# Longer steps in the second group: 16 ticks before the last attention products of six heads, ten between retention steps

## The chip, the cores and the metric

The kernel runs on one core of a Trainium2 chip. The metric is the device time of one execution in microseconds (us). A core has five engines with a queue of their own: TensorE (PE, with its weight loads as PEld), VectorE (DVE), ScalarE (ACT), GpSimd (POOL) and SyncE (SP), which here only issues transfers. Each engine takes its instructions in order; semaphores make it wait for another.

## The reference

One step of a layer with two groups of eight heads, head size 128, on 1024 prompt rows and 8 streams of 16 sample rows with 1024 cached rows each. All is in 32 bits.

```python
q_sb, k_sb, v_sb, gate_sb, q_r, k_r, v_r, gate_r = project(rms_norm(x), w_in)   # 2048 x 8192, rope on q_r, k_r
# stick-breaking attention: z = q k^T / sqrt(128), strictly causal
a = exp(log_sigmoid(z) + later)        # later: sum of log_sigmoid(-z) over the keys that follow
o_sb = a @ v
# retention: chunks of 64, a state s per head
o_r = (q k^T * intra) @ v + (q @ s) * decay_read
s = s * exp(lg * n) + k^T @ (decay_write * v)
y = concat(head_rms_norm(o_sb) * silu(gate_sb), head_rms_norm(o_r) * silu(gate_r))
x = x + rms_norm(y @ w_out)
```

It returns the new rows of x, the new keys and values, and the retention states.

## The kernel before

**Groups and panels.** The prompt's rows are eight tiles of 128. The first group takes tiles 0 to 3 and the sample rows, the second tiles 4 to 7. In each group a loop goes over the eight heads; a head has panels: queries, keys and gate of retention (`ret_queries`, `ret_keys`, `ret_gate`), queries and keys of attention and, for two heads at a time, its values (`attention`), and the gate (`gates`). Every weight block comes as `wr` through SP (L215, L271 for row panels, L1020 for the output), is split by ScalarE (L131, `wh`) and VectorE (L132, `wl`) into two parts, and is used in three products (L229, L288 in row panels, L1030 to L1032 in the output). In the second group a panel has 48 products of 128x512 and a row panel 192 of 128x256. After the groups come four output panels for three chunks of row tiles; the first of them still runs with ticks.

**Jobs and ticks.** All other work is in jobs, Python generators that run beside the panels. After each product of a panel (each three of a row panel, four times after each tile's three products in the first output panel) `tick()` raises a clock by one and lets at most one job do its next step: the one that is due. What a step yields is the number of ticks until the job is due again. `drain(job)` ticks without products until a job is done.

```python
def tick():
    clock[0] += 1
    for job in jobs:
        if job.at <= clock[0]:
            wait = step(job)
            ...
            job.at = clock[0] + wait
```

The constants D_... hold these numbers, mostly as pairs for the two groups (`phase[0]` is 0 or 1). The ticks fix the order in which the program is written down; a scheduler may still move an instruction within its engine's order, so that one which isn't ready stands a little later.

**The attention job** (`stick_breaking`, L562 to L623) takes a head's four row tiles through six steps. Step s makes the scores of row s (L588, into rotating PSUM banks), sigmoids on ScalarE (L500, L501), masks on GpSimd (L506), the scan and the multiplication on VectorE (L517, L518), and sends `be` to DRAM block by block (L474). One step later it is read back (L481), so that the blocks are exchanged; two steps later VectorE transposes within the blocks (L578). Then come the products with the values (L618, one pair of passes for each of the row's tiles, into the one PSUM bank `pa`), a copy (L621) and a sum of squares (L538). In steps 4 and 5, which make no scores, a yield of D_TR ticks (L612) stands between the transpose of row 2 or 3 (t = 6 or 7, seven or eight tiles) and its products. In the second group the job also has D_NAT 11, D_TB 24 and D_AV 11 ticks in its steps. `finish` scales the rows and turns them through DRAM (L474 on ScalarE's queue, L481 on SP's), 23 and 13 ticks apart.

**The retention job** (`ret_branch`, `retention`, L747 to L800) turns the keys the same way (L474, L481, L851), and then takes four chunks. For each: scores of the next chunk (L754, `rs`) and their decay on VectorE (L756, `sc`), products with the values and with the state (L772, L777, into `pa`), two combining instructions (L780, L781); then, D_RET ticks later, the product for the new state (L787, `pS`) and its update on VectorE (L792); and D_RET ticks later the next chunk. So there are nine yields of D_RET in the second group.

```python
sc = scores(0, 0)
yield D_RET[phase[0]]
for i in range(4):
    nxt = scores(i + 1, 0)
    ...
    yield D_RET[phase[0]]
    ...
    yield D_RET[phase[0]]
```

**The end of a job.** The next head drains the retention job after its retention queries' panel, and the attention job after its attention queries' panel (the last head both after the first output panel). In heads 5 to 7 of the second group the panels come in another order: heads 5 and 6 have attention earlier, and head 7 begins with it; the time until the drain is 256 ticks for the attention jobs of heads 4 and 5, and 304 for those of heads 0 to 3 and 6.

**The seam.** At the start of the second group the decode job of the first group's last head, which attends to the cached rows (L661, L728 with values from `vc`, L689), ends beside the first retention of the second group.

## Time and profile before

| what | us |
|---|---|
| median of three runs (2395.4 to 2400.91) | 2400.34 |
| the profiled execution | 2397.79 |
| its span, first to last instruction | 2396.1 |
| its TensorE busy / VectorE / ScalarE / GpSimd | 2332.6 / 1254.6 / 919.6 / 646.2 |
| mean granted TensorE clock | 0.993 of full |

A row of the timeline has the start in us, the duration, the engine, the line, the operation, the tiles (written<-read), the shape and the count of equal instructions that follow each other; in brackets, how long the engine was idle before it and what ended that. A row of the table by stretches has the stretch, its length, each engine's busy time and instructions in the order PE, PEld, DVE, ACT, POOL, then the granted clock, the share of the DMA engines' time and GB/s. A row of waits has the waiting line, what it waited for, the sum in us, how often, and the longest.

### The profile page before, as it was taken

To read this page: it belongs to the slowest core of one execution; us is meant where nothing else is said; L and a number is where in the kernel's file an instruction comes from. 1 tells how busy PE (TensorE), PEld (TensorE's weight loads), DVE (VectorE), ACT (ScalarE), POOL (GpSimd) and SP (SyncE) were. 2 spreads that over 40 slices of the span, in tenths; PEclk is the share of its full clock that TensorE was granted. 3 is DMA by queue.
4 is the path that set the end of the run, shared out by engine and by line. 5 is a ranking of instruction groups with operands and counts; after the bars stand their busy time and mean duration, and the time that the engine had idled before them with its cause. 6 is when DMAs were issued, how large, how long until landed. Compare 5 with 4: busy or idle time off the path is not lost.

```text
span 2396.1 us, 40529 instructions
## 1 busy us (share of the span) xinstructions
PE 2332.6 (97%) x14832; PEld 2094.6 (87%) x14832; DVE 1254.6 (52%) x2442; ACT 919.6 (38%) x1937; POOL 646.2 (27%) x1033
## 2 busy tenths in 40 slices
PE   7999999999999999998899999999999999999998
PEld 7998899999999999987778888889898888888887
DVE  7245455445554555455545554555554566564544
ACT  6323333324333333324333343343343444444443
POOL 3144353444344353443302111120220220010000
PEclk9999999999999999999999999999999999999999
DMA  7658879797889879798875555556654667765553
GB/s 244 166 130 210 167 166 197 174 199 164 188 178 191 181 174 187 182 192 199 188 189 150 150 141 150 146 142 153 153 152 127 166 163 195 231 214 181 189 191 131
DMA packets 677050, 418.68 MB, mean 175 GB/s; under 512 B 224753, under 2 KB 620017, under 8 KB 674545
## 3 DMA queue, kind: packets, MB, share of 16 engines
q1 hardware_dynamic: 524272, 285.99, 47.6%
q0 software_dynamic: 32256, 71.36, 13.7%
q10 hardware_dynamic: 120320, 58.74, 9.0%
q8 instruction: 116, 1.90, 0.3%
q14 instruction: 86, 0.70, 0.1%
HBM read 336.24 MB, written 79.69 MB: 174 GB/s over the span
## 4 chain that ended last, share of the span: by engine, by line
PE 83%; DMA 7%; DVE 4%; issue 2%; ACT 2%; SPq 1%; POOL 0%; DVEq 0%; ACTq 0%; POOLq 0%
PE acc L229 44%; PE accn L288 17%; DMA mr<-s_y 4%; PE a L1031 3%; PE a L1032 3%; PE a L1030 3%; PE pa L618 3%; PE z L588 2%; DMA wr<-w_in 2%; PE zc L661 1%; PE pd L728 1%; DMA mr<-s_h 1%; DVE wl L132 1%; DVE ml L132 1%; ACT mh L131 1%
## 5 line engine op out<-in xcount | busy, mean ns | idle before, releaser
L229 PE MATMUL acc<-mh,wh 128*128 128x256 f32 (+2 forms) x2304 | 665.4, 342 | 7.8 <-ACT wh L131 5.0
L132 DVE TENSOR_TENSOR wl<-wr,wh 128x512 fp32r<-128x512 f32 (+1 forms) x576 | 391.8, 685 | 523.8 <-ACT wh L131 513.8
L229 PE MATMUL acc<-ml,wh 128*128 128x384 f32 (+2 forms) x2304 | 663.8, 341 | 0.0
L229 PE MATMUL acc<-mh,wl 128*128 128x256 f32 (+2 forms) x2304 | 660.2, 339 | 0.6 <-DVE wl L132 0.5
L131 ACT ACTIVATE wh<-wr 128x512 fp32r<-128x512 f32 (+1 forms) x576 | 357.4, 625 | 730.9 <-PE acc L229 247.7
L229 PEld LDWEIGHTS acc<-mh,wh 128*128 128x128 f32 x2304 | 420.7, 189 | 45.0 <-ACT wh L131 7.1
L229 PEld LDWEIGHTS acc<-mh,wl 128*128 128x128 f32 x2304 | 424.7, 189 | 31.6 <-issue 2.1
L229 PEld LDWEIGHTS acc<-ml,wh 128*128 128x128 f32 x2304 | 422.9, 189 | 33.2 <-issue 5.3
L645 POOL DMA_DIRECT2D kc<-cache_sb_k x512 | 331.6, 653 | 370.0 <-DVE kcT L683 205.9
L288 PE MATMUL accn<-whn,mh 128*128 128x256 f32 x1152 | 329.2, 287 | 0.6 <-ACT whn L131 0.5
L288 PE MATMUL accn<-wln,mh 128*128 128x256 f32 x1152 | 325.9, 283 | 1.5 <-DVE wln L132 1.5
L288 PE MATMUL accn<-whn,ml 128*128 128x256 f32 x1152 | 325.9, 283 | 0.0
L288 PEld LDWEIGHTS accn<-whn,mh 128*128 128x128 f32 x1152 | 220.5, 192 | 10.5 <-issue 7.5
L288 PEld LDWEIGHTS accn<-wln,mh 128*128 128x128 f32 x1152 | 220.9, 192 | 2.5 <-DVE wln L132 1.7
L288 PEld LDWEIGHTS accn<-whn,ml 128*128 128x128 f32 x1152 | 220.9, 192 | 0.0
L1031 PE MATMUL a<-wl,mh 128*128 128x512 f32 (+1 forms) x576 | 219.5, 381 | 0.2 <-DVE wl L132 0.2
L1032 PE MATMUL a<-wh,ml 128*128 128x512 f32 (+1 forms) x576 | 219.0, 381 | 0.0
L1030 PE MATMUL a<-wh,mh 128*128 128x512 f32 (+1 forms) x576 | 218.9, 381 | 0.0
L132 DVE TENSOR_TENSOR wln<-wrn,whn 128x512 fp32r<-128x512 f32 x128 | 87.5, 687 | 119.7 <-ACT whn L131 119.5
L131 ACT ACTIVATE whn<-wrn 128x512 fp32r<-128x512 f32 x128 | 80.1, 633 | 151.6 <-PE accn L288 65.4
L481 POOL DMA_DIRECT2D be<-s_be x128 | 94.0, 741 | 134.2 <-DMA s_be<-be 114.6
L1031 PEld LDWEIGHTS a<-wl,mh 128*128 128x128 f32 x576 | 108.4, 188 | 21.2 <-DVE wl L132 0.9
(189 smaller groups left out, 2611.6 us busy)
## 6 DMA issues: line engine op xcount, KB each, us to landing
wr<-w_in SPq DMA_DIRECT2D x384, 256.0 KB, 4.2
wr<-w_out SPq DMA_DIRECT2D x184, 256.0 KB, 3.6
wrn<-w_in SPq DMA_DIRECT2D x128, 256.0 KB, 3.2
kc<-cache_sb_k POOLq DMA_DIRECT2D x512, 64.0 KB, 4.6
vc<-cache_sb_v SPq DMA_DIRECT2D x64, 512.0 KB, 8.5
xt<-x_prompt SPq DMA_DIRECT2D x8, 1024.0 KB, 6.2
xr<-x_prompt SPq DMA_DIRECT2D x8, 1024.0 KB, 6.5
out<-out ACTq DMA_DIRECT2D x24, 256.0 KB, 3.6
```

Source lines behind the costliest of these rows:

```text
L131: nc.scalar.activation(hi, src, AF.Copy)
L132: nc.vector.tensor_tensor(lo, src, hi.bitcast(F32), ALU.subtract)
L229: last = nc.tensor.matmul(a[:, :m], lhs[:, j, :], rhs[w][:, j, o : o + m], start=(w == 0 and j == 0 and n == 0), stop=(w == KT // WQ - 1 a ...
L288: anchor[0] = nc.tensor.matmul(a, lhs[q][:, jj, ts], rhs[:, j, :], start=(w == 0 and j == 0 and n == 0 and t % 2 == 0), stop=(w == KT // 2 ...
L481: q.dma_start(raw[32 * i : 32 * i + 32, :].rearrange("p (k a) -> p k a", a=32), s[:, :, 32 * i : 32 * i + 32].rearrange("k (j b) a -> b (k ...
L588: nc.tensor.matmul(z[:, :c], q2[a][:, i * P : (i + 1) * P], k2[b][:, s : s + c], start=(m == 0), stop=(m == 2),)
L618: nc.tensor.matmul(po[:, :P], at[:, j, :], vn[:, j, :], start=(j == 0), stop=(j == t))
L645: nc.gpsimd.dma_start(kc[32 * i : 32 * i + 32, :].rearrange("p (k d) -> p k d", d=32), cache_k[0, 2 * c + j, s * 512 : (s + 1) * 512, h, 3 ...
L661: mm = nc.tensor.matmul(z[r, :], qp[:, j, r], ready[2 * j + c // 2][:, c % 2, :], start=(j == 0), stop=(j == 1),)
L1030: nc.tensor.matmul(a[:, :width], hi[q][:, j, ts], wh, start=(k == 0), stop=False)
L1031: nc.tensor.matmul(a[:, :width], hi[q][:, j, ts], wl, start=False, stop=False)
L1032: nc.tensor.matmul(a[:, :width], lo[q][:, j, ts], wh, start=False, stop=(k == KT - 1))
```

## The change

D_TR gets a third number, 16, and D_RET of the second group goes from 5 to 10. In the second group the attention job of heads 4 and 5 (H - 4 and H - 3) keeps the 7 ticks before the products of rows 2 and 3; the other six heads get 16. The decode job, which uses D_TR too, belongs to the first group and keeps its 3. Nothing that is computed changes.

```diff
-D_TR = (3, 7)
+D_TR = (3, 7, 16)
...
-D_RET = (9, 5)
+D_RET = (9, 10)
...
                     if step >= len(todo) and (early or step > len(todo)):
-                        yield D_TR[phase[0]]
+                        yield D_TR[phase[0] and (1 if h in (H - 4, H - 3) else 2)]
                     while "vn" not in rest:
                         yield 3
```

## The prediction

> **What bounds the kernel now.** I read the page first, then the table by stretches, then the list of waits of TensorE for the second group alone, and last the timeline at each of those waits.

> ```profile
> PE 2332.6 (97%) x14832; PEld 2094.6 (87%) x14832; DVE 1254.6 (52%) x2442; ACT 919.6 (38%) x1937; POOL 646.2 (27%) x1033
> ```
> ```profile
> 1205.00:1230.00 25.00, 20.01 (x137) 14.46 (x137) 11.65 (x30) 8.59 (x22) 0.00 (x0) 0.93 0.78 199
> 1230.00:1960.00 730.00, 723.35 (x4115) 634.12 (x4114) 389.40 (x673) 288.26 (x595) 132.22 (x208) 1.00 0.58 150
> 1960.00:2010.00 50.00, 48.17 (x252) 40.39 (x251) 37.01 (x77) 27.66 (x64) 13.32 (x16) 1.00 0.75 198
> 2010.00:2396.00 386.00, 375.85 (x1792) 316.56 (x1790) 196.61 (x354) 161.68 (x344) 19.03 (x11) 0.99 0.59 190
> ```

> TensorE is busy 97% of the span. The two new constants act in the second group only, which is roughly 1205 to 2010 us here, and in what it hands to the output panels behind it. In the body of the group (730 us) TensorE is not busy for 730.00 - 723.35 = 6.65 us; in its last 50 us for 1.83 us. So even a perfect change there can't give more than some 8.5 us plus what lies in the 25 us at the seam of the groups. That is the first bound: 0.4% at most.

> ```profile
> PE pa L618 <- DVE kp L578: 5.0, 6, 1.1
> PE pa L772 <- DVE so L621: 1.1, 1, 1.1
> PE acc L229 <- DVE rk L325: 1.0, 1, 1.0
> PE pS L787 <- DVE rkn L855: 0.7, 1, 0.7
> PE pa L772 <- DVE sc L756: 0.6, 1, 0.6
> ```

> This is the whole list of TensorE's waits from 1225 to 2010 us (total us, times, longest). The change aims at the first row: products of attention rows (L618) that wait for VectorE's transpose (L578). The other four are in the retention of the last heads.

> **The change part by part.** A step waits in ticks; a tick is one product of a panel (or one group of three in a row panel). Ten products lie between these two starts:

> ```profile
> 1199.80 0.39 PE L229 MATMUL acc<-ml,wh 128*128 128x512 f32 x1
> 1202.07 0.38 PE L754 MATMUL rs<-rq,rk 128*128 128x128 f32 x2
> 1202.20 0.48 PE L229 MATMUL acc<-mh,wl 128*128 128x512 f32 x1
> 1202.52 0.40 PE L229 MATMUL acc<-mh,wh 128*128 128x512 f32 x1
> ```

> (1202.07 - 1199.80) / 10 = 0.227 us a product, so nine more ticks are 2.04 us. A pair of small products between panels costs 0.13 us until the next product, which itself takes 0.32 instead of 0.227: about 0.22 us. The change adds and removes no instruction: 13720 matmuls stand on TensorE in both builds. It only moves them, and spreads the small groups of the second group over 178 places instead of 170; as the pair above costs no more than its own passes, I take the extra splitting as 0.

> *Attention rows.* Here are the six waits of the first row, one each for heads 0 to 5.

> ```profile
> 1303.12 1.83 PE L618 MATMUL pa<-vn,kp 128*128 128x128 f32 x14 [1.06 <-DVE kp L578]
> 1402.98 1.16 PE L618 MATMUL pa<-vn,kp 128*128 128x128 f32 x8 [0.66 <-DVE kp L578]
> 1510.85 1.83 PE L618 MATMUL pa<-vn,kp 128*128 128x128 f32 x14 [1.06 <-DVE kp L578]
> 1610.72 1.16 PE L618 MATMUL pa<-vn,kp 128*128 128x128 f32 x8 [0.66 <-DVE kp L578]
> 1718.58 1.83 PE L618 MATMUL pa<-vn,kp 128*128 128x128 f32 x14 [1.06 <-DVE kp L578]
> 1808.68 1.83 PE L618 MATMUL pa<-vn,kp 128*128 128x128 f32 x14 [0.54 <-DVE kp L578]
> ```

> All are the row of seven tiles; the row of eight never waits. Heads 4 and 5 keep their 7 ticks, so 1.06 + 0.54 stay. For the rest I compared the built order of TensorE's instructions, counted in panel products. In heads 1 and 3 the row moves nine products later (from product 7756 to 7765, and 8716 to 8725). In heads 0 and 2 it stands at the same product in both builds (7293 and 8253), and its transpose follows the same instructions on VectorE: there the longer step moves nothing, and 2 x 1.06 us stay. Heads 6 and 7 are not in the list: nothing to win.

> Whether nine products are enough in heads 1 and 3 depends on VectorE:

> ```profile
> 1395.14 0.69 DVE L132 TENSOR_TENSOR wl<-wr,wh 128x512 fp32r<-128x512 f32 x1 [1.89 <-ACT wh L131]
> 1398.30 2.28 DVE L517 TENSOR_TENSOR_SCAN kp<-kp 128x1024 f32<-128x1024 f32 x1
> 1400.68 1.22 DVE L518 TENSOR_TENSOR be<-be,kp 128x1024 f32<-128x1024 f32 x1
> 1401.83 1.10 DVE L578 STREAM_TRANSPOSE kp<-be 128x896 f32<-128x896 f32 x1
> ```

> The transpose stands behind the scan and the multiplication of the next row, 4.6 us in all. In the changed build a copy and one weight split (0.69 us) come ahead of that scan, so I shift the transpose's end from 1402.93 to about 1403.9. TensorE came to the row at 1402.98 - 0.66 = 1402.32 and will come at 1402.32 + 2.04 = 1404.36. That is 0.4 us behind the transpose, so both waits go: **-1.3 us**. The bounds: 0 if the shift is 1.5 us or more, -3.4 us if all four waits of the changed heads went.

> *Retention.* Four waits of the last two heads:

> ```profile
> 1889.95 0.49 PE L772 MATMUL pa<-rv,sc 128*128 128x128 f32 x2 [0.64 <-DVE sc L756]
> 1958.78 0.47 PE L229 MATMUL acc<-mh,wh 128*128 128x512 f32 x1 [0.97 <-DVE rk L325]
> 1976.02 0.46 PE L787 MATMUL pS<-rv,rkn 128*128 128x128 f32 x2 [0.70 <-DVE rkn L855]
> 1983.81 0.49 PE L772 MATMUL pa<-rv,sc 128*128 128x128 f32 x2 [1.14 <-DVE so L621]
> ```

> The first stood directly behind its scores; in the changed build four panel products and an attention group come between (0.9 us and more against 0.64): -0.64. The third moves nine products later: -0.70. The second is the rope of a panel and stays. The fourth stays too: the attention group whose copy it waits for still stands four products ahead of it. Bounds for these four: 0 to -3.4; I take **-1.3 us**. Everywhere else in the group retention's five ticks already cost no wait in the list, so ten can't win anything there. The steps end 45 ticks (10 us) later, but the next head drains the job 240 ticks or more after its start and it needs 173, so no drain meets it. What moves on SP with them are the loads that turn its output (L481), and they block the weight loads behind them:

> ```profile
> SPq L481 <- DMA s_o<-ro: 20.2, 7, 6.8
> ```

> Seven heads wait there, up to 6.8 us, and no wait for weights is in TensorE's list: the weights split ahead cover it. Without that cover a wait like this one would cost up to 6.8 us a head. In the built order of SP these loads stand at most six weight loads later, with the next weights behind them as before, so I take 0.

> *The seam of the groups.* Here the first retention of the group and the last products of the decode (L728) share a wait for weights:

> ```profile
> 1208.81 1.14 SPq L689 DMA_DIRECT2D vc<-cache_sb_v  x2
> 1219.82 0.79 PE L229 MATMUL acc<-mh,wh 128*128 128x512 f32 x1 [4.68 <-ACT wh L131]
> 1227.70 1.07 PE L728 MATMUL pd<-vc,kp 128*32 128x256 f32 x16
> 1228.70 0.51 PE L229 MATMUL acc<-mh,wh 128*128 128x512 f32 x1
> ```

> SP's order up to these weight loads is unchanged, so TensorE again starts on them at about 1219.8. What changes is what lies in the shadow of the wait. Before, three pairs of retention and the last 16 passes of L728 stood behind it: 3 x 0.22 + 1.0 = 1.7 us. In the changed build 10 of those 16 passes stand in the shadow, and behind it the other 6 and seven pairs of retention: 0.4 + 7 x 0.22 = 1.9 us. **+0.2 us**. Those ten passes need the last two value loads, issued by 1209.9 and therefore ahead of the weights in the same queue, which bounds their cost by 0 to about 1 us.

> The same wait also drops the clock:

> ```profile
> 1219.82:1223.00 3.18, 3.18 (x9) 2.60 (x10) 2.96 (x7) 2.24 (x6) 0.00 (x0) 0.50 0.85 230
> 1113.28 2.85 PE L815 MATMUL pa<-st,rq 128*32 128x256 f32 x8 [2.38 <-DMA st<-state_ret]
> 1113.82:1117.23 3.41, 3.41 (x11) 1.57 (x11) 0.23 (x1) 0.27 (x1) 3.41 (x6) 0.50 1.09 319
> ```

> Nine products took 3.18 us at a granted clock of 0.50, against 9 x 0.227 = 2.04 at full: 1.1 us. In the changed build the ten passes cut the idle 4.68 us into pieces of some 2 us. A gap of 2.38 us at 1113 already brought 0.50, so by the rows I leave the drop in: 0, bounds 0 and -1.1. [...]

> **The sum**: -1.3 - 1.3 + 0.2 = -2.4 us. On the profiled execution's own time, 2397.79 us (span 2396.1), that is 2395.4. The median of the runs shown is 2400.34, 2.55 above it; from there the forecast is 2397.9 us, 0.1% below. A measurement of this kernel can tell about 0.3% (7.2 us) from no change, so this is inside.

> **The rivals.**

> *It does all that it says*: the waits of heads 0 and 2 go too (-2.1). For it: the diff gives those heads 16 ticks. Against it: the row stands at the same product in the built order. -4.5 us, 2395.8.

> *The clock holds at the seam*: the ten passes break the idle time into pieces too short to lower it. For it: the largest piece halves. Against it: the gap of 2.38 us above. -2.4 - 1.1 = -3.5 us, 2396.8. [...]

> *Nothing arrives*: the weight split ahead of the scan waits for ScalarE, as the one at 1395.14 did for 1.89 us. Then the transpose ends near 1405.8, TensorE comes at 1404.36 and waits 1.4 us instead of 0.66 in heads 1 and 3. It decides from a split wait of 0.4 us. -2.4 + 1.3 + 1.5 = +0.4, 2400.7.

> *Slower*: the end of the last head. In the changed build two loads of the moving operand (mr) stand ahead of the second output weight in SP's queue, and their splits with them.

> ```profile
> 1980.97 1.00 ACT L131 ACTIVATE mh<-mr 128x384 fp32r<-128x384 f32 x2 [1.57 <-DMA mr<-s_y]
> 1992.73 1.14 ACT L131 ACTIVATE wh<-wr 128x512 fp32r<-128x512 f32 x2
> 1995.88 0.39 PE L1030 MATMUL a<-wh,mh 128*128 128x512 f32 x1
> ```

> The first of these two splits ends near 1993.3, and its weight is used at 1995.88: a cushion of 2.5 us. Two more pairs at 1.00 us and one wait like the 1.57 each make 1.00 + 2 x 1.57 = 4.1: 1.6 us late, and a gap there may bring half clock for one stretch as at 1219 (+1.1), while retention's 0.70 is lost. If several weights of this panel are hit in turn, four times 1.6. One hit: -2.4 + 0.7 + 1.6 + 1.1 = +1.0 us, 2401.3; four hits with the clock: +5.8, 2406.1. It decides from 2.5 us of extra wait ahead of that split. Against it: these weights are issued in good time now, and the list of TensorE's waits names none for them.

> **How the numbers follow.** Forecast 0.50; all that it says 0.10; the clock holds 0.12; nothing arrives 0.15; slower 0.13. The runs of before scatter from 2395.4 to 2400.91, about 2.5 to either side, and that comes on top of each case. Eight in ten: from 2395.8 less 2.5 to the single hit at 2401.3 plus 2.5, that is 2393.3 to 2403.8. Faster by over 0.3% (below 2393.1) needs nearly every wait of the group and the clock: 0.07. Slower by over 0.3% (above 2407.5) needs four hits and more: 0.06. Within: 0.87.

> **What the changed profile would show.** Right: TensorE's list of waits for L618 on L578 falls from 5.0 us in six to about 3.7 in four (1.06 three times, 0.54); the rows on sc and rkn are gone; those on so (L621) and rk (L325) remain; the wait for weights near 1219.8 keeps its end. Wrong: waits of 0.5 us or more at L618 in heads 1 and 3 (then VectorE's order ate the nine products), a new row for L1030 or L1031 near 1995, or a clock near 1.0 in the stretch behind 1219.8. If the body's busy gap stays at 6.65 us, the forecast's mechanism is wrong even if the time fits.

## The result, and the profile after

The changed kernel takes 2401.6 us (median of 22 runs, 2396.8 to 2411.8) against 2397.3 for the kernel before (22 runs on the same chip, 2392.1 to 2404.2): a ratio of 1.002, 95% interval 1.0012 to 1.0027, or +4.3 us by the medians (2.9 to 6.5 by the interval). So the change is slower by a little more than the measurement's uncertainty. The time lies inside the forecast's range and within 0.3% of the kernel before, but the sign is wrong: -2.4 us was forecast. The profiled execution took 2406.4 us (span 2404.7).

Busy time on the page after, then the table by stretches, cut where the group and the panels end now:

```profile
PE 2339.6 (97%) x14832; PEld 2098.5 (87%) x14832; DVE 1257.3 (52%) x2442; ACT 911.4 (38%) x1933; POOL 647.8 (27%) x1033
```
```profile
1205.00:1230.00 25.00, 19.84 (x125) 12.92 (x124) 11.57 (x30) 7.52 (x17) 0.00 (x0) 0.86 0.81 199
1230.00:1960.00 730.00, 725.47 (x4126) 634.88 (x4125) 386.80 (x669) 284.42 (x595) 136.53 (x207) 1.00 0.58 148
1960.00:2015.00 55.00, 52.22 (x269) 43.51 (x268) 40.70 (x76) 27.19 (x64) 12.32 (x17) 1.00 0.82 203
2015.00:2404.00 389.00, 376.98 (x1789) 317.17 (x1788) 198.84 (x360) 159.30 (x347) 16.98 (x11) 0.99 0.60 189
```

The body, cut by time, looks better than before: 730.00 - 725.47 = 4.53 us not busy, where it was 6.65. About 1 us of that is only the cut: the rope's wait of 0.97 us ended at 1958.78 before, inside the body, and its successor ends at 1965.27, behind it. The list of TensorE's waits in the group is shorter too (total us, times, longest):

```profile
PE pa L618 <- DVE kp L578: 4.3, 5, 1.1
PE acc L229 <- DVE rk L325: 1.8, 1, 1.8
PE pS L787 <- ACT mh L131: 0.9, 1, 0.9
```

8.4 us of waits have become 7.0. But the output panels behind the group, where the kernel before had one wait of 0.2 us, have two rows:

```profile
PE a L1030 <- ACT wh L131: 1.7, 1, 1.7
PE a L1031 <- DVE wl L132: 0.9, 1, 0.9
```

To see where the time went I counted panel products. Both kernels make the same 12,096, in the same order but for 21 that stand a few places off between 10286 and 10437, so the time from product m to product n can be compared wherever it lies in the span. The table holds means of three profiles of each kernel, from three executions, since one is not enough: products 1 to 6860 (the first group, where the two builds are the same) took 1171.3 to 1178.9 us. The last two columns are single profiles of two experiments.

| products, what | before | after | difference | forecast | attention alone | 30/16 steps |
|---|---|---|---|---|---|---|
| 6860-6960, seam | 39.4 (38.4 to 40.1) | 40.8 (40.4 to 41.4) | +1.4 | +0.2 | 40.2 | 39.2 |
| 7180-7440 and 7960-8410, heads 0, 2 | 174.4 | 174.5 | +0.1 | 0 | 174.4 | 172.4 |
| 7440-7960 and 8410-8930, heads 1, 3 | 215.7 | 215.4 | -0.3 | -1.3 | 213.8 | 215.2 |
| 9332-9960, head 5 | 114.7 | 115.6 | +0.9 | 0 | 114.7 | 114.7 |
| 10030-10190 | 45.7 | 45.3 | -0.4 | -0.6 | 45.8 | 45.8 |
| 10190-10300, rope of head 7's keys | 29.2 | 31.6 | +2.4 | 0 | 29.4 | 29.2 |
| 10300-10460, last retention | 50.0 | 48.7 | -1.3 | -0.7 | 50.6 | 50.2 |
| 10700-11100, output panels | 91.0 | 93.9 | +2.9 | 0 | 91.8 | 90.7 |
| 6860-12090, all behind the first group | 1167.1 | 1172.4 | +5.3 | -2.4 | 1167.8 | 1164.1 |

What isn't listed differs by -0.2. The sum of +5.3 lies inside the measured interval of 2.9 to 6.5. One shift between two rows has to be set right: three score products of the last head (L588, 0.7 us in all) stand in the rope's stretch in the changed kernel and in the last retention's before. So the rope pays 1.7 us and not 2.4 (0.6 of it is half clock in one of the three profiles), and the last retention gives 0.6 and not 1.3. The waits in the body did get shorter, and three places that the prediction held to be free, or nearly, pay for it: the seam, one rope, and the output panels 150 us after the group.

### The profile page after: what moved, and what is told of

It is laid out like the page before. It is cut to its first block, busy times and chain, and to the rows that moved or that the text cites. A ratio compares the mean times of both kernels' runs of the same rounds, so it can differ in the third digit from the quotient of the medians.

```text
span 2404.7 us, 40520 instructions
## 1 busy us (share of the span) xinstructions
PE 2339.6 (97%) x14832; PEld 2098.5 (87%) x14832; DVE 1257.3 (52%) x2442; ACT 911.4 (38%) x1933; POOL 647.8 (27%) x1033
## 4 chain that ended last, share of the span: by engine, by line
PE 80%; DMA 8%; DVE 4%; issue 3%; POOL 2%; ACT 2%; SPq 1%; ACTq 0%; DVEq 0%; POOLq 0%
PE acc L229 41%; PE accn L288 17%; PE a L1030 4%; PE a L1031 4%; PE a L1032 4%; DMA mr<-s_y 4%; PE pa L618 3%; PE z L588 2%; DMA wr<-w_in 1%; PE pd L728 1%; PE zc L661 1%; POOL kc L645 1%; DMA mr<-s_h 1%; DVE wl L132 1%; DMA kb<-s_be 1%
## 5 line engine op out<-in xcount | busy, mean ns | idle before, releaser
L229 PE MATMUL acc<-mh,wh 128*128 128x256 f32 (+2 forms) x2304 | 666.1, 342 | 4.5 <-DVE rk L325 1.8
L229 PE MATMUL acc<-ml,wh 128*128 128x384 f32 (+2 forms) x2304 | 664.4, 341 | 0.0
L229 PE MATMUL acc<-mh,wl 128*128 128x256 f32 (+2 forms) x2304 | 659.7, 339 | 0.6 <-DVE wl L132 0.5
L132 DVE TENSOR_TENSOR wl<-wr,wh 128x512 fp32r<-128x512 f32 (+1 forms) x576 | 390.8, 685 | 507.8 <-ACT wh L131 504.2
L131 ACT ACTIVATE wh<-wr 128x512 fp32r<-128x512 f32 (+1 forms) x576 | 355.8, 624 | 714.2 <-PE acc L229 244.9
L229 PEld LDWEIGHTS acc<-mh,wh 128*128 128x128 f32 x2304 | 421.3, 189 | 42.0 <-issue 8.4
L229 PEld LDWEIGHTS acc<-mh,wl 128*128 128x128 f32 x2304 | 424.9, 189 | 31.8 <-issue 2.1
L229 PEld LDWEIGHTS acc<-ml,wh 128*128 128x128 f32 x2304 | 423.5, 189 | 33.2 <-issue 5.3
L1030 PE MATMUL a<-wh,mh 128*128 128x512 f32 (+1 forms) x576 | 220.2, 382 | 1.8 <-ACT wh L131 1.7
L1031 PE MATMUL a<-wl,mh 128*128 128x512 f32 (+1 forms) x576 | 219.9, 382 | 0.9 <-DVE wl L132 0.9
L132 DVE TENSOR_TENSOR wln<-wrn,whn 128x512 fp32r<-128x512 f32 x128 | 87.5, 690 | 121.3 <-ACT whn L131 120.3
L131 ACT ACTIVATE whn<-wrn 128x512 fp32r<-128x512 f32 x128 | 80.3, 633 | 146.1 <-PE accn L288 66.5
L481 POOL DMA_DIRECT2D be<-s_be x128 | 94.3, 743 | 135.9 <-DMA s_be<-be 119.8
L1030 PEld LDWEIGHTS a<-wh,mh 128*128 128x128 f32 x576 | 108.8, 189 | 23.3 <-ACT wh L131 2.2
```

The costliest lines, as they stand in the source:

```text
L131: nc.scalar.activation(hi, src, AF.Copy)
L132: nc.vector.tensor_tensor(lo, src, hi.bitcast(F32), ALU.subtract)
L229: last = nc.tensor.matmul(a[:, :m], lhs[:, j, :], rhs[w][:, j, o : o + m], start=(w == 0 and j == 0 and n == 0), stop=(w == KT // WQ - 1 a ...
L481: q.dma_start(raw[32 * i : 32 * i + 32, :].rearrange("p (k a) -> p k a", a=32), s[:, :, 32 * i : 32 * i + 32].rearrange("k (j b) a -> b (k ...
L1030: nc.tensor.matmul(a[:, :width], hi[q][:, j, ts], wh, start=(k == 0), stop=False)
L1031: nc.tensor.matmul(a[:, :width], hi[q][:, j, ts], wl, start=False, stop=False)
```

## The experiments

At first three theories stood against each other: **A**, the seam (longer half clock); **B**, the output panels; **C**, accidents of one execution. Then: **D**, retention of heads 6 and 7 (rope and panels), **E**, attention of heads 6 and 7, **F**, spreading retention costs by itself. All ratios are to the kernel before on the same chip.

### The seam alone, all but the seam, and new profiles

```diff
 # retention of head 0 alone at ten
-            yield D_RET[phase[0]]
+            yield D_RET[phase[0] and (2 if h == 0 else 1)]     # D_RET = (9, 5, 10)
 # the changed kernel, head 0's retention at five
+            yield D_RET[phase[0] and (2 if h > 0 else 1)]
```

> The kernel before with ten ticks between the retention steps of head 0 of the second group alone; in the built order of TensorE only the seam of the groups differs (products 6860 to 6960), and it is that of the changed kernel there. Theory A (the loss is at the seam: the small products that used to fill the wait for weights now come behind it, and the half clock lasts 6.8 us instead of 3.4): the stretch from product 6860 to 6960 takes about 40.5 us instead of 38.4, and the run is slower than before by about 2 us (0.1%). Theory B (the loss is in the output panels, where TensorE waited 2.6 us for split weights near 2151 us and lost 1.4 us more to the clock): no difference, the stretch near 2151 us has no wait. Theory C (both are accidents of one execution): the seam takes 38.4 us.

> The changed kernel with five ticks for head 0's retention: the seam stands as before, everything else as in the changed kernel. Theory A: the seam takes 38.4 us again, and the run is within 1 us of before. Theory B: slower than before by about 4 us, with a wait of TensorE for split weights near 2145 us. Theory C: no difference, no wait there.

> The changed kernel again, for a second profile. Theory A: the seam takes 40.5 us again. Theory B: the wait near 2150 us is there again, 2.6 us and half clock behind it. Theory C: one or both are gone.

> The kernel before again, for a second profile. Theories A and B: the seam takes 38.4 us, and no wait near 2145 us. Theory C: one of the two shows here as well.

Head 0 alone: 2397.5 us, 1.0006 (0.9996 to 1.0017), the seam at 41.0 us. All but head 0: 2401.0 us, 1.0026 (1.0014 to 1.0038), the seam at 40.3. The changed kernel again: 1.0017 (1.0005 to 1.0028), seam 41.4, panels' stretch 11040 to 11100 at 16.6 us (18.4 in the first profile, 13.9 before). The kernel before again: one execution of 2396.2 us, seam 39.6. So A is a small part at most: the loss stays without it. B is there in both profiles, smaller the second time.

### Attention alone, and retention by heads

```diff
 # attention alone: the change's D_TR, D_RET = (9, 5)
 # retention of heads 1 to 5 alone at ten, attention as before
+            yield D_RET[phase[0] and (2 if 0 < h < H - 2 else 1)]
 # retention of heads 6 and 7 alone at ten, attention as before
+            yield D_RET[phase[0] and (2 if h >= H - 2 else 1)]
 # both parts in heads 0 to 5 (retention 1 to 5, attention 0 to 3)
+            yield D_RET[phase[0] and (2 if 0 < h < H - 2 else 1)]
+                        yield D_TR[phase[0] and (1 if h >= H - 4 else 2)]
```

> The kernel before with the 16 ticks ahead of the last attention products of six heads, retention left at five. In the built order SP and GpSimd are as before, and the output panels too. Theory D (the loss comes with the retention steps of heads 6 and 7: they push the last head's scores and scans ahead of its rope, about +1 us of wait and in some executions half clock, and give the moving loads of the output panels other places among the weights, +1 to +4 us): no loss here; the waits at L618 in heads 1 and 3 fall from 0.66 to 0.15 us, and the run is within 1.5 us of before, rather below. Rival E (the longer attention steps of heads 6 and 7 are what makes the end late): slower by 2 us or more, with waits near 1958 or 2145 us.

> The kernel before with ten ticks between the retention steps of heads 1 to 5 of the second group alone. Theory D and rival E: within 1 us of before, and no new wait of TensorE over 0.5 us. Rival F (spreading retention costs by itself, a little at each of its steps): slower by 1 us or more, spread over 1310 to 1750 us.

> The kernel before with ten ticks between the retention steps of heads 6 and 7 alone. Theory D: slower by 3 to 5 us; the wait for the rope (L325) near 1958 us is near 1.8 us, and TensorE waits in the output panels between 2080 and 2165 us. Rivals E and F: within 1 us of before.

> The change kept where it loses nothing by theory D: 16 ticks for the attention of heads 0 to 3, ten for the retention of heads 1 to 5, all else as before. Theory D: 1 us below before (the two waits at L618), nothing in the output panels; below the changed kernel by 4 to 6 us. Rival F: 1 us or more above before.

Attention alone: 2393.2 us, **0.999 (0.9981 to 0.9999)**, faster than both kernels, though the interval only just excludes no change. (Its column in the table doesn't show the gain: the profiled execution, 2397.7 us, was one of the two slowest of eleven.) Retention of heads 1 to 5: 2399.5, 1.0016 (1.0004 to 1.0028). Retention of heads 6 and 7: 2401.6, **1.0021 (1.001 to 1.0033)**, which is as much as the whole loss of the change. Both parts in heads 0 to 5: 2395.5, 1.000 (0.9989 to 1.0011), which decides nothing between 1 us less and 1 us more. The parts add up to more than the whole, 0.06 + 0.16 + 0.21 - 0.10 = 0.33% against 0.2%, but each is uncertain by 0.1%. E falls; D holds for the sum, F for heads 1 to 5.

### Which of the last two heads, and the loads' queue

```diff
+            yield D_RET[phase[0] and (2 if h == H - 2 else 1)]   # head 6; h == H - 1 for head 7
 # the changed kernel, the output chunks' moving loads on GpSimd's queue
-            nc.sync.dma_start(r, src(k))
+            queue.dma_start(r, src(k))          # nc.gpsimd when called from fetch (L1010)
```

> The kernel before with ten steps of retention in head 6 alone. Theory 'round trip': VectorE now has retention's L551 and L552 between the scan and the rope of head 7, so that the row's transposition (L578, which reads be back from the DMA) comes right behind the sum and waits for the transfer, ahead of the rope of head 7's keys. Then the products behind the rope (6th stretch of the table, small products 10190 to 10300) take 31.2 us against 29.1 to 29.5, as with heads 6 and 7 together, and TensorE's wait at the first of them is about 1.8 us against 0.6 to 1.0; the output panels of the second chunk lie at other weights too, with +0 to +2.5 us. In all +2 to +4.5 us, 1.001 to 1.002. Rival 'head 7': both losses come with head 7's retention; then this run is at 1.000 and the stretch at 29.3 us.

> The kernel before with ten steps of retention in head 7 alone. VectorE's order around the rope of head 7's keys is that of the kernel before, but the loads of the moving tiles stand at other weights of the output panels. Theory 'round trip' plus 'panels': the rope's stretch stays at 29.3 us, and the stretch of the second chunk's first output panel (products 11040 to 11100) takes 16 us or more against 14.0; +2 us or a little more, 1.001. Rival 'panels by chance': the order in the last 130 weights is as before in all that matters, and the longer stretch of the changed kernel comes from the state of the loads in one execution; then 14.0 us here and 1.000. Rival 'head 7': rope and panels are both late; 1.002.

> The changed kernel, but the loads of the moving tiles for the second and third chunk of the output (L207 as called from L1010) are issued by GpSimd in place of SyncE; nothing else. Theory 'queue': in the changed kernel ScalarE waits 4.6 us for such a load at 2148 us, with the splits of the weights queued behind it, because SyncE issues it behind five weight loads that wait for buffers (11.1 us). With a queue of its own the load is there in time, the stretch of products 11040 to 11100 falls from 16.6 us (mean of three profiles) to 14.0 or less, and about 2.5 us of the changed kernel's loss are gone: 1.001 against the kernel before. Rival 'buffers': the load waits for its own two buffers, whichever queue issues it; then the stretch stays at 15 to 18 us and the ratio at 1.002. Rival 'GpSimd's order': the waiting loads hold up the additions (L1093) that GpSimd does for the rows' ends; then slower than the changed kernel, 1.003 or more.

Head 6: 2397.8, 1.0009 (0.9999 to 1.0019); rope 31.1 us, panels' stretch 15.3, but the last retention gives back 1.4. Head 7: 2398.7, 1.0011 (1.0 to 1.0022); rope 29.4 us, panels' stretch 16.6. So the rope's loss belongs to head 6 and both heads disturb the panels. GpSimd's queue: 2419.5, **1.0099 (1.0083 to 1.0116)**: my theory of the queue fell, and both of its rivals have a row (waits of GpSimd, then of ScalarE, behind 2020 us):

```profile
POOL out L1093 <- ACT out L1092: 225.6, 9, 102.7
POOL mr L207 <- DVE ml L132: 117.5, 42, 37.2
```
```profile
ACT mh L131 <- DMA mr<-s_y: 71.5, 43, 5.3
```

The loads wait on GpSimd for a buffer that the splits must free (42 times; on SyncE 31 times, 28.4 us), and behind GpSimd's own additions, which wait up to 102.7 us for ScalarE. ScalarE waits no less for them (60.4 us in 34 waits in the changed kernel): another queue does not get them there earlier.

### More steps, and a set for each pair of heads

```diff
 # 30 steps in heads 0 to 3, retention at five
+                        yield D_TR[phase[0] and (2 if h < H - 4 else 1)]          # D_TR = (3, 7, 30)
 # 30 in heads 0 and 2, 16 in heads 1 and 3, retention at five
+                        yield D_TR[phase[0] and (1 if h >= H - 4 else 2 if h % 2 else 3)]   # (3, 7, 16, 30)
```

> The kernel before with one edit: in heads 0 to 3 of the second group the last attention row waits 30 product steps between transposition and products; retention stays at 5 and the last four heads stay as they were. Theory 'rows': with the attention change alone heads 1 and 3 each got 0.97 us shorter, because the wait at the row's products went. At 16 steps the row of heads 0 and 2 stayed at the same product and kept its wait of 1.06 us; at 30 it moves 6 products on. So heads 1 and 3 give 0.97 each and heads 0 and 2 up to 1.06 each: -4.0 us in the profile's stretches, a ratio of 0.998 and about 2391 us. Rival 'only odd heads': the wait of heads 0 and 2 hangs on VectorE's place in the order and not on the number of products between; then -1.9 us, 0.999, as with the attention change alone. Rival 'the row holds up the next head': the later products push the next head's first row; then 1.000 or above.

> The kernel before with the last attention row's wait set by head: 30 product steps in heads 0 and 2 of the second group, 16 in heads 1 and 3, the rest as before; retention stays at 5. Theory 'rows': the two gains add, 1.02 us each in heads 0 and 2 (as with 30 steps in all four heads) and 0.97 each in heads 1 and 3 (as with 16), -4.0 us in the table's stretches and 2392 us, 0.998 against the kernel before. Rival 'pushed on': the later row of heads 0 and 2 moves VectorE's work of the next heads, and heads 1 and 3 lose what they had gained; then -2 us, 0.999.

> The changed kernel once more, for another profile. Theory 'order': the seam stays above the mean of the unchanged order (39.5 us), at 40.3 to 41.4; the rope's stretch is 31 us with one wait, or 32.7 with a half clock behind it; the first output panel of the second chunk takes 15 to 18 us. Rival 'accident': seam 38 to 40, panel 13.6 to 14.8.

> The kernel before once more, for another profile. Theory 'order': seam 38 to 40.2 us, rope 29.1 to 29.5, panel 13.6 to 14.8. Rival 'accident': one of the three is in the changed kernel's range (seam 41 or more, rope 31 or more, panel 15 or more).

30 steps: 2392.4 us, **0.9989 (0.998 to 0.9997)**. Heads 0 and 2 give the expected 1.0 us each, heads 1 and 3 only 0.2. The mixed set: 2394.0, 0.9987 (0.9974 to 1.0001), the same picture: heads 1 and 3 give 0.2 with 16 steps as well. "Pushed on" was right. Its waits in the group, and VectorE at the start of head 1:

```profile
PE pa L618 <- DVE kp L578: 1.6, 2, 1.1
...
PE acc L229 <- DVE wl L132: 0.8, 2, 0.4
```
```profile
1349.56 1.58 DVE L517 TENSOR_TENSOR_SCAN kp<-kp 128x640 f32<-128x640 f32 x1 [3.23 <-POOL kp L506]
1351.06 0.66 DVE L132 TENSOR_TENSOR wl<-wr,wh 128x512 fp32r<-128x512 f32 x1
```

All four waits of heads 0 to 3 at L618 are gone (the two left are heads 4 and 5). But a weight split now stands behind head 1's first scan, which waits 3.23 us for GpSimd's mask, and TensorE waits 0.41 us for that split, once each in heads 1 and 3, over half of the 0.7 us that each of them gives back. The three versions with attention alone can't be told apart; each is 0.1% ahead of the kernel before (the mixed set's interval reaches 1.0001).

The two last profiles: the changed kernel at 2398.9 us with seam 40.4, rope 31.0, panels' stretch 13.6; the kernel before at 2392.3 with 40.1, 29.1, 13.6. For the rope "order" holds; for the panels this profile of the changed kernel speaks for "accident", which the next section weighs.

## Why the prediction was wrong, step by step

The steps that failed are those that priced the surroundings of the longer retention steps at nothing or nearly: the rope that "stays" cost 1.7 us, the output panels taken as 0 cost 2.9, the seam 1.4 instead of 0.2, and of the 1.3 us forecast for the attention rows 0.3 came, because retention moved VectorE's order there too. One by one:

**Heads 0, 2, 4: right.** The rows stood at the same product and kept 1.06 us each.

**Attention rows, -1.3: the mechanism was right, the size was not.** TensorE at L618 in the changed kernel, heads 3 and 5 (head 1's wait is as short as head 3's, and falls just out of the list):

```profile
1616.66 1.16 PE L618 MATMUL pa<-vn,kp 128*128 128x128 f32 x8 [0.15 <-DVE kp L578]
...
1813.34 1.83 PE L618 MATMUL pa<-vn,kp 128*128 128x128 f32 x14 [1.00 <-DVE kp L578]
```

VectorE ahead of head 1's row in the changed kernel:

```profile
1403.75 0.69 DVE L132 TENSOR_TENSOR wl<-wr,wh 128x512 fp32r<-128x512 f32 x1 [0.62 <-ACT wh L131]
1404.36 2.28 DVE L517 TENSOR_TENSOR_SCAN kp<-kp 128x1024 f32<-128x1024 f32 x1
1406.75 1.23 DVE L518 TENSOR_TENSOR be<-be,kp 128x1024 f32<-128x1024 f32 x1
1407.89 1.11 DVE L578 STREAM_TRANSPOSE kp<-be 128x896 f32<-128x896 f32 x1
```

I had shifted the transposition by one weight split and a copy, and priced the split's wait for ScalarE as a rival that decides from 0.4 us. It waits 0.62, so TensorE is 0.15 us early at the row where I had it 0.4 us late (and not the rival's 1.4 early). Retention's ten steps put that split there: with attention alone L618 has no wait in heads 1 and 3 and each gives 0.94 us; with retention alone the wait there is 1.05 instead of 0.66, and each loses 0.7:

```profile
1403.90 1.83 PE L618 MATMUL pa<-vn,kp 128*128 128x128 f32 x14 [1.05 <-DVE kp L578]
```

Counted by products, the row itself (7740 to 7780) gives 0.95 with attention alone, costs 0.4 with retention alone and gives 0.5 with both. Behind it (7820 to 7920) the same retention pairs between other products cost 0.34 more wherever retention takes ten steps, with or without attention's: this I had taken as 0. So 0.16 a head are left. The two halves of the change work against each other, and head 5, which keeps its 7 steps, pays 1.00 instead of 0.54, half of its +0.9; another 0.3 is the last pair of head 4's retention (L787), which now falls into this stretch. "Everywhere else ten can't win" was right; that it can lose was missing.

**Retention's waits, -1.3: near in size, half of it by luck.** Measured is -1.0 (-0.4, and -0.6 in the last retention). The wait on the scores went. The wait on `rkn`, which I had counted as gone, stayed at 0.9 (the first and third profile name `mh`, the second `rkn`); the wait on `so` (1.0 to 1.6 us in the three profiles before), which I had counted as staying, went. In the third profile of the changed kernel TensorE waits at the first output panel instead (at 1988 us, for VectorE's part of the gate). That is the row near 1995 that the prediction named as a sign of being wrong:

```profile
PE a L1030 <- DVE rg L315: 1.4, 1, 1.4
```

(The prediction's 13720 matmuls is not the pages' count, which is 14832 in both kernels; that none is added holds.)

**The rope "stays": wrong.** The wait was 0.97 us (0.58 and 0.59 in the other two profiles before) and is 1.78 (1.94 and 1.78). The first fence is VectorE before, the second VectorE of the changed kernel, the third VectorE with head 6 alone:

```profile
1953.19 1.75 DVE L517 TENSOR_TENSOR_SCAN kp<-kp 128x768 f32<-128x768 f32 x1
...
1957.96 0.68 DVE L325 TENSOR_TENSOR rk<-acc,cosT 128x512 f32<-128x512 f32 x1
1958.56 2.01 DVE L517 TENSOR_TENSOR_SCAN kp<-kp 128x896 f32<-128x896 f32 x1
```
```profile
1959.32 3.76 DVE L517 TENSOR_TENSOR_SCAN kp<-kp 128x768 f32<-128x768 f32 x2
1962.99 0.93 DVE L518 TENSOR_TENSOR be<-be,kp 128x768 f32<-128x768 f32 x1
1963.84 0.68 DVE L324 TENSOR_TENSOR sw<-sw,sinT 128x512 f32<-128x512 f32 x1
1964.44 0.68 DVE L325 TENSOR_TENSOR rk<-acc,cosT 128x512 f32<-128x512 f32 x1
```
```profile
1953.35 0.84 DVE L578 STREAM_TRANSPOSE kp<-be 128x640 f32<-128x640 f32 x1 [2.04 <-DMA be<-s_be]
...
1955.39 0.68 DVE L325 TENSOR_TENSOR rk<-acc,cosT 128x512 f32<-128x512 f32 x1
```

Before, one scan stood ahead of the rope and the other behind it. In the changed kernel two scans stand ahead of it. With head 6 alone the order differs again: the transposition meets its transfer too early and waits 2.04 us. Both ways the rope is late, and TensorE's next products, which need what it frees, wait 0.7 to 1.4 us longer. Head 7 alone leaves the order and the wait as they were. TensorE in the changed kernel's first and second profile, and with head 6 and head 7 alone:

```profile
1965.27 0.47 PE L229 MATMUL acc<-mh,wh 128*128 128x512 f32 x1 [1.78 <-DVE rk L325]
```
```profile
1956.39 0.47 PE L229 MATMUL acc<-mh,wh 128*128 128x512 f32 x1 [1.94 <-DVE rk L325]
```
```profile
1956.22 0.47 PE L229 MATMUL acc<-mh,wh 128*128 128x512 f32 x1 [1.69 <-DVE rk L325]
```
```profile
1957.00 0.47 PE L229 MATMUL acc<-mh,wh 128*128 128x512 f32 x1 [0.92 <-DVE rk L325]
```

**The seam, +0.2: the clock's sign was wrong.** The ten passes did fall in the shadow of the wait, and its end stayed, on average: the product behind it (6888) starts 19.3 us behind product 6860 with either order (17.6 to 20.3 in twelve profiles, 19.05 to 19.55 in five). The profile that I argued from was an early one, 18.4. The changed kernel, and the clock there:

```profile
1217.53 0.64 PE L728 MATMUL pd<-vc,kp 128*32 128x256 f32 x8 [1.49 <-DMA vc<-cache_sb_v]
1221.26 0.94 PE L728 MATMUL pd<-vc,kp 128*32 128x256 f32 x2 [3.09 <-DMA vc<-cache_sb_v]
1222.78 0.79 PE L229 MATMUL acc<-mh,wh 128*128 128x512 f32 x1 [0.58 <-ACT wh L131]
1223.93 1.08 PE L728 MATMUL pd<-vc,kp 128*32 128x256 f32 x6
1224.94 0.80 PE L754 MATMUL rs<-rq,rk 128*128 128x128 f32 x2
```
```profile
1221.42:1228.24 6.82, 6.24 (x19) 3.42 (x18) 4.34 (x12) 4.50 (x8) 0.00 (x0) 0.50 0.86 235
```

TensorE waits 1.49 + 3.09 + 0.58 = 5.2 us in pieces (4.68 in one before), the two long ones for the value loads themselves, and half clock lasts 6.8 us. My bounds for the clock were 0 and -1.1: I had not thought that it could last longer. It lasted 3.4 us in two, 6.8 in nine and 10.2 in one of the twelve profiles with the seam as before (37.6 to 40.9 us, mean 39.7), 6.8 in two and 10.2 in three of the five with the changed seam (40.4 to 41.4, mean 40.9). The profile that I argued from had one of the two short ones. That is about +1.2 us between the means. Behind product 6888 the clock is at half for 5.6 us on average with the changed seam and for 4.3 with the other, and half of that difference, 0.6, is lost (at 0.50 products start 0.43 us apart, at full clock 0.23); the work that now stands there takes 0.45 us more, where I had 0.2. The run with head 0 alone (+1.4, interval -1.0 to +4.1) fits without proving it.

**The output panels at 0: wrong.** My rival "slower" had the mechanism (moving loads at other places among the weights of SP's queue) but put it at 1993 us. It hits the second chunk's first panel. ScalarE, SP and TensorE of the changed kernel, and the clock behind:

```profile
2142.59 0.63 ACT L131 ACTIVATE wh<-wr 128x512 fp32r<-128x512 f32 x1 [2.75 <-DVE wl L132]
2147.86 0.42 ACT L131 ACTIVATE mh<-mr 128x256 fp32r<-128x256 f32 x1 [4.64 <-DMA mr<-s_y]
...
2150.29 0.61 ACT L131 ACTIVATE wh<-wr 128x512 fp32r<-128x512 f32 x1
```
```profile
2131.82 11.10 SPq L1020 DMA_DIRECT2D wr<-w_out  x5
2143.01 0.92 SPq L207 DMA_DIRECT2D mr<-s_y  x2
```
```profile
2150.95 0.49 PE L1030 MATMUL a<-wh,mh 128*128 128x512 f32 x1 [1.74 <-ACT wh L131]
...
2152.33 0.50 PE L1031 MATMUL a<-wl,mh 128*128 128x512 f32 x1 [0.89 <-DVE wl L132]
```
```profile
2153.26:2156.66 3.40, 3.40 (x10) 2.61 (x9) 1.46 (x4) 1.54 (x4) 1.29 (x1) 0.50 0.91 246
```

On ScalarE the split of the moving block waits 4.64 us for its load, and the weight's split (2150.29), which TensorE needs, stands behind it. SP and ScalarE before, at the same place:

```profile
2125.76 10.07 SPq L1020 DMA_DIRECT2D wr<-w_out  x5
2135.92 0.86 SPq L207 DMA_DIRECT2D mr<-s_y  x2
```
```profile
2140.62 0.60 ACT L131 ACTIVATE mh<-mr 128x256 fp32r<-128x256 f32 x2
```

Before, the two loads are issued 8.7 us ahead of the product in question (11043, at 2144.57), and the split doesn't wait for them. In the changed kernel they are issued 6.2 us ahead of the time when TensorE is ready for it (2150.95 - 1.74 = 2149.21). The two waits and the half clock make this stretch 18.4 us. From the 56th weight on, ScalarE's and SP's orders are those of before; what differs are the places of the moving loads among the 30 weights ahead of that, and so how far the splits are ahead. That the last heads' retention sets it is shown: of the seven profiles that spread it in head 6, 7 or both (GpSimd's queue apart) six have waits of 0.8 us or more here (stretch 14.9 to 18.4), and none of the nine others has more than 0.5 (13.6 to 14.8). The seventh, the third profile of the changed kernel, has the same order and none (13.6): the cushion is thin, not gone. How the places of the loads thin it is argued, not shown, and the one attempt to take the cause away failed.

## What to carry to other kernels

In a schedule where jobs share one clock, a step that is made longer has its price wherever its last tick lands, here up to 150 us later, in a queue order that no wait of the kernel before points to: compare the built order of each in-order engine and of the DMA queue behind the change, and give the cushions there a price even when the profile shows no wait. Two constants that each move VectorE's order should be tried apart: attention alone gained 0.1%, together with retention it lost 0.2%. And where a stretch ends on a wait that may drop the clock (half clock lasted 3.4 to 10.2 us behind the seam's), take more than one profile before costing it.

## What the runs showed of the hardware that was not expected

The granted clock fell to 0.50 after waits still shorter than the 2.38 us that the prediction quotes. At the rope's products, idle times of 1.69, 1.78, 1.78 and 1.79 us left it at full, and 1.93, 1.93 and 1.94 were followed by 3.4 us at half each (here the second profile of the changed kernel, 1.94):

```profile
1956.93:1960.34 3.41, 3.41 (x10) 2.64 (x9) 2.84 (x5) 0.00 (x0) 1.28 (x2) 0.50 0.56 193
```

The price is more than the list of waits shows: a wait of 1.94 us makes the rope's stretch 32.7 us where 1.78 makes it 31.0.
